# A two-block kernel: the input's pieces loaded in another order, and fourteen matmuls of ones at the head

## The chip, the core and the metric

One core of a Trainium2 chip runs the whole program. Its engines are TensorE (PE, matmuls; its weight loads are PEld), VectorE (DVE), ScalarE (ACT), GpSimd (POOL) and SyncE (SP, which issues most of the DMA transfers). Each engine works through its own list of instructions in order and waits at an instruction until what it needs is there. The metric is the device time of one execution, in microseconds (us). In the profiled execution the span, from the first instruction to the last, is a little shorter than that time.

## What is computed

The reference is two transformer-like blocks over 256 positions of width 1024, one after the other. Here matters the start of the first one:

```python
def first_block(x, mem, mix_norm_g, w_in, ...):
    ...
        h = _rmsnorm(x, mix_norm_g[l])
        proj = h @ w_in[l]
        u_s5, q_in, k_in, v_in, o_in, i_pre, f_pre, gate_pre = jnp.split(proj, split_points, axis=-1)
        y_s5 = _s5(u_s5, ...)          # complex diagonal scan, 32 groups of 64 states
        y_m = _mlstm(q_in, k_in, v_in, o_in, i_pre, f_pre, ...)   # gated matrix memory, 4 heads, 2 chunks of 128
        ...
        merged = g_s5 * (y_s5 @ w_br_s5[l]) + g_m * (y_m @ w_br_m[l])
        x = x + merged @ w_out[l]
        h = _rmsnorm(x, x_norm_g[l])
        x = x + _cross_attn(h, _rmsnorm(mem, mem_norm_g[l]), x_wq[l], x_wkv[l], x_wo[l])
        h = _rmsnorm(x, f_norm_g[l])
        x = x + _conv_ffn(h, f_w_up[l], f_conv_w[l], f_conv_b[l], f_w_down[l])
    return _rmsnorm(x, final_norm_g)
```

The second block has two layers of attention and convolution networks. All values are float32.

## The kernel before

Products with weights are made from pairs. `wload` (L313) fetches a weight tile by SP into `raw`, ScalarE casts it to `hi` (L321) and VectorE makes `lo` = raw - hi (L322). The activations have such a pair too, `xh` (ScalarE, L569) and `xl` (VectorE, L570). A product is then three matmuls, hi with xh, hi with xl, lo with xh: `fm_mm` (L329 to L331, the result has features on the partitions) and `tm_mm` (L338 to L340, it has positions there). The pool for `raw` has 4 buffers, those for `hi` and `lo` 3 each, and the PSUM tiles `g` for the results 3; `a` (4) and `m` (1) are the other PSUM tiles.

The head fetches the first weight tile in two halves of 512 columns and the input `x` in four pieces of 2 of its 8 slices (L1653 to L1667). `rms_defer` (L566) makes xh and xl from the unnormalised x, slice by slice, and squares, a sum by matmuls with a column of `ones` (`col_sums`, L455) and a broadcast (L499) for the norm's factor, which is multiplied in later where results leave PSUM (L1689, `msg`). The order of the first long part is then: products for the scan's input and for q and k (`w_fm`, L329 to L331, with the convolution L1695 to L1700 behind them), the scan's tables (VectorE's `so` and `hs`, L754 and L755; ScalarE's L764 to L790; TensorE's L779 to L787), products for v, the two gates and the output gate (`w_vif` and `w_tm`, L338 to L340; `ifs` at L1716, `vm` at L1714, `og` at L1729 and L1730), the scan's local sums (L805, evicted by ScalarE L806), the scan over time on VectorE (L815 to L818), and the mLSTM (from L888; per head L919, L928, ScalarE's `dm`, VectorE's `pT` L931, then L933 to L935; `hn` L951; L952), with further `w_fm` products, which need none of these, in between. The scan's output is L842, from 155 us.

The order of the instructions isn't the program's. `tile.TileContext(schedule_with_timeline_sim=True)` lets a scheduler place them by priorities and by a time that it computes itself, so a change of a priority, or of the work at the head, can move instructions far behind it. `tc.high_priority(n)` raises what stands under it by n; `wload` raises its own by `WPRI` = 300 within whatever stands around it.

Of the kernel before, what the change touches and what calls it, by code (L numbers as in the profile page):

```python
# [20 lines left out]
P = 128  # L21
# [10 lines left out]
WPRI = 300  # L32
# [220 lines left out]
def program(tc, nc, a, offs, dump=lambda n, t: None):  # L253
    with ExitStack() as ctx:
        _program(ctx, tc, nc, a, offs, dump)


def _program(ctx, tc, nc, a, offs, dump):
# [14 lines left out]
    pm = pool(ctx, "pm", 1, space=PSUM)  # L273
    cnt = [0]

    def T(pl, shape, tag, dt=F32, **k):
        cnt[0] += 1
        return pl.tile(list(shape), dt, tag=tag, name="%s_%d" % (tag, cnt[0]), **k)
# [6 lines left out]
    mm = PE.matmul  # L285
# [4 lines left out]
    ident = C["ident"]  # L290
    ones = T(cp, [P, P], "ones")
    G.memset(ones, 1.0)
    mhalf = T(cp, [P, 8], "mhalf")
    G.memset(mhalf, -0.5)
    zcol = T(cp, [P, 1], "zcol")
# [17 lines left out]
    def wload(name, i, c0=0, c1=None):  # L313
        src = a[name][i]
        src = src[:, c0:src.shape[-1] if c1 is None else c1]
        n = src.shape[-1]
        with tc.high_priority(WPRI):
            raw = T(wr, [P, n], "raw")
            nc.sync.dma_start(raw, src)
            hi, lo = [T(next(wp[s]), [P, n], s, F32R) for s in ("hi", "lo")]  # L320
            ACT.copy(hi, raw)  # L321
            tt(lo, raw, hi, op=sub)  # L322
        return hi, lo
# [1328 lines left out]
    with ExitStack() as ph:  # L1652
# [3 lines left out]
        with tc.high_priority(1000):  # L1656
            nc.scalar.dma_start(early, a["early"])

            first = []
            for half_ in range(2):  # L1660
                with tc.high_priority(4000 - WPRI):
                    first.append(wload("w_fm", 0, 512 * half_, 512 * half_ + 512))
                for k in range(2 * half_, 2 * half_ + 2):
                    with tc.high_priority(4000):
                        nc.sync.dma_start(x[:, 2 * k:2 * k + 2, :], a["x"][:, 2 * k:2 * k + 2, :])
            ahead = [([(0, 4), (4, 4)], first)]
            C.update({k: early[:, o:o + n] for k, (o, n) in off_e.items()})  # L1667
# [181 lines left out]
```

## Time and profile before

| what | value |
| --- | --- |
| time, median of 3 runs | 1207.07 us (1204.92 to 1209.34) |
| time of the profiled execution | 1207.08 us |
| its span | 1205.3 us |
| mean granted clock of TensorE | 0.991 |
| TensorE busy | 1165.0 us (97%) |
| VectorE busy | 888.5 us (74%) |
| ScalarE busy | 692.3 us (57%) |
| GpSimd busy | 73.1 us (6%) |

Busy times are sums over the span. An engine's share tells little of a stretch, as the stretches have different limits; a time outside the span (1207.08 - 1205.3 = 1.8 us) belongs to no instruction.

### The profile page before, as it was taken

Reading aid. Unit: us, or ns where it says so; the run is one execution under the profiler, and the core shown is the slowest. Engines: PE = TensorE matmul, PEld = TensorE weight load, DVE = VectorE, ACT = ScalarE, POOL = GpSimd, SP = SyncE. Lnnn points to the kernel's source line nnn. Section 1 sums busy time; section 2 is a strip of 40 time slices with the busy share of each in tenths; the row PEclk is TensorE's granted clock in tenths of the full one; section 3 lists DMA queues with packets and bytes.
Section 4 is the critical chain, followed back from the end, with each engine's and each line's share of the span. In section 5 each row is a group of like instructions: output and inputs, shape, how many; then the busy total and the mean of one; then the engine's idle time right before and its main releaser. Section 6 shows DMA issues by size and latency. Waiting matters only on the chain.

```text
span 1205.3 us, 23538 instructions
## 1 busy us (share of the span) xinstructions
PE 1165.0 (97%) x9370; PEld 1106.2 (92%) x9370; DVE 888.5 (74%) x1685; ACT 692.3 (57%) x1229; POOL 73.1 (6%) x80
## 2 busy tenths in 40 slices
PE   7899999999999999999999899999999999999997
PEld 7889989999999998899988899998988789999986
DVE  8979857866688887667565886666697868976654
ACT  5684645655565765446355675554686666755441
POOL 4400000100000000000001000001000001000010
PEclk9999999999999999999999999999999999999998
DMA  7524435654356556656433466666863225666561
GB/s 269 156 73 154 159 117 186 215 184 140 122 166 203 180 184 174 196 180 213 163 92 108 160 186 182 179 182 190 296 202 107 67 74 184 203 191 178 161 204 36
DMA packets 61276, 199.41 MB, mean 165 GB/s; under 512 B 8502, under 2 KB 12398, under 8 KB 60910
## 3 DMA queue, kind: packets, MB, share of 16 engines
q1 hardware_dynamic: 54864, 191.60, 50.1%
q10 hardware_dynamic: 6302, 6.32, 1.6%
q8 instruction: 73, 1.20, 0.4%
q14 instruction: 37, 0.30, 0.1%
HBM read 196.28 MB, written 1.60 MB: 164 GB/s over the span
## 4 chain that ended last, share of the span: by engine, by line
PE 87%; DVE 6%; ACT 3%; issue 2%; DMA 1%; POOL 1%; DVEq 0%; SPq 0%; ACTq 0%
PE g L330 12%; PE g L329 12%; PE g L331 12%; PE a L329 7%; PE a L330 7%; PE a L331 7%; PE a L394 5%; PE g L394 4%; PE a L396 3%; PE g L340 2%; PE g L338 2%; PE g L339 2%; DVE lo L322 2%; PE g L396 2%; PE m L1150 1%
## 5 line engine op out<-in xcount | busy, mean ns | idle before, releaser
L322 DVE TENSOR_TENSOR lo<-raw,hi 128x1024 fp32r<-128x1024 f32 (+3 forms) x359 | 428.4, 1199 | 181.9 <-ACT hi L321 179.5
L321 ACT CAST hi<-raw 128x1024 fp32r<-128x1024 f32 (+3 forms) x359 | 363.6, 1020 | 341.5 <-PE g L330 127.7
L329 PE MATMUL g<-xh,hi 128*128 128x256 f32 (+1 forms) x616 | 176.0, 286 | 8.3 <-ACT xh L569 8.0
L330 PE MATMUL g<-xl,hi 128*128 128x256 f32 (+1 forms) x624 | 178.3, 286 | 0.3
L331 PE MATMUL g<-xh,lo 128*128 128x256 f32 (+1 forms) x616 | 175.3, 285 | 1.4 <-DVE lo L322 1.4
L329 PE MATMUL a<-nh,hi 128*128 128x256 f32 x560 | 159.4, 285 | 4.7 <-ACT sqa L1075 2.8
L330 PE MATMUL a<-nl,hi 128*128 128x256 f32 x560 | 158.8, 284 | 0.9 <-DVE nl L517 0.9
L331 PE MATMUL a<-nh,lo 128*128 128x256 f32 x560 | 158.7, 284 | 0.0
L329 PEld LDWEIGHTS g<-xh,hi 128*128 128x128 f32 x616 | 117.2, 190 | 9.6 <-ACT xh L569 8.0
L330 PEld LDWEIGHTS g<-xl,hi 128*128 128x128 f32 x624 | 118.9, 190 | 1.6 <-DVE xl L570 0.8
L331 PEld LDWEIGHTS g<-xh,lo 128*128 128x128 f32 x616 | 116.9, 190 | 2.4 <-DVE lo L322 2.0
L329 PEld LDWEIGHTS a<-nh,hi 128*128 128x128 f32 x560 | 108.1, 193 | 5.7 <-ACT sqa L1075 2.9
L330 PEld LDWEIGHTS a<-nl,hi 128*128 128x128 f32 x560 | 108.1, 193 | 1.1 <-DVE nl L517 1.1
L331 PEld LDWEIGHTS a<-nh,lo 128*128 128x128 f32 x560 | 108.0, 193 | 0.0
L394 PE MATMUL a<-mx,hi 128*128 128x512 f32 x264 | 91.9, 394 | 0.0
L329 PE MATMUL g<-nh,hi 128*128 128x256 f32 x288 | 81.5, 283 | 0.0
L330 PE MATMUL g<-nl,hi 128*128 128x256 f32 x288 | 81.5, 283 | 0.0
L331 PE MATMUL g<-nh,lo 128*128 128x256 f32 x288 | 81.5, 283 | 0.0
L396 PE MATMUL a<-mx,lo 128*128 128x256 f32 x264 | 73.1, 277 | 0.0
L394 PE MATMUL g<-mx,hi 128*128 128x512 f32 x198 | 69.0, 395 | 0.0
L394 PEld LDWEIGHTS a<-mx,hi 128*128 128x128 f32 x264 | 49.4, 188 | 11.5
L329 PEld LDWEIGHTS g<-nh,hi 128*128 128x128 f32 x288 | 55.3, 192 | 0.0
(619 smaller groups left out, 2863.8 us busy)
## 6 DMA issues: line engine op xcount, KB each, us to landing
raw<-g_up SPq DMA_DIRECT2D x88, 512.0 KB, 3.6
raw<-f_up SPq DMA_DIRECT2D x44, 512.0 KB, 3.5
raw<-g_dn SPq DMA_DIRECT2D x32, 512.0 KB, 3.6
raw<-w_fm SPq DMA_DIRECT2D x27, 512.0 KB, 3.7
raw<-ev_fm SPq DMA_DIRECT2D x20, 512.0 KB, 3.7
raw<-f_dn SPq DMA_DIRECT2D x16, 512.0 KB, 3.5
raw<-od_fm SPq DMA_DIRECT2D x14, 512.0 KB, 4.4
raw<-g_dn SPq DMA_DIRECT2D x16, 384.0 KB, 3.3
```

Of the source, the lines that this page charges most:

```text
L321: ACT.copy(hi, raw)
L322: tt(lo, raw, hi, op=sub)
L329: mm(ps, hi[:, o:o + P], xh[:, k, :], start=start and k == 0, stop=False, skip_group_check=skip)
L330: mm(ps, hi[:, o:o + P], xl[:, k, :], start=False, stop=False, skip_group_check=skip)
L331: mm(ps, lo[:, o:o + P], xh[:, k, :], start=False, stop=stop and k == kt - 1, skip_group_check=skip)
L338: mm(ps, xh[:, k, t], hi[:, wsl], start=start and j == 0, stop=False, skip_group_check=skip)
L339: mm(ps, xh[:, k, t], lo[:, wsl], start=False, stop=False, skip_group_check=skip)
L340: mm(ps, xl[:, k, t], hi[:, wsl], start=False, stop=stop and j == len(ks) - 1, skip_group_check=skip)
L394: mm(f2, hi[:, o], X[:, k].rearrange("p a s -> p (a s)"), start=first and j == 0, stop=False, skip_group_check=True)
L396: mm(ps[:, 0, :], lo[:, o], X[:, k, 0, :], start=False, stop=last and j == len(ks) - 1, skip_group_check=True)
L1150: mm(o[64 * r:64 * r + 64, :], v0, pT[:, 0:S], start=first, stop=False, skip_group_check=True)
```

## The change

A PSUM tile `warm` is taken from the pool of `m`, and 14 matmuls of the tile `ones` (128x128, float32) with itself are written into it, as soon as `ones` is set; nothing reads it. And the priorities of the six transfers at the head change: the second half of the weight tile gets 100 less than the first, and each piece of x a number of its own, falling from the first to the last. Other numbers are not touched.

```diff
     ones = T(cp, [P, P], "ones")
     G.memset(ones, 1.0)
+    warm = T(pm, [P, P], "m")
+    for _ in range(14):
+        mm(warm, ones, ones, start=True, stop=True)
     mhalf = T(cp, [P, 8], "mhalf")
...
             for half_ in range(2):
-                with tc.high_priority(4000 - WPRI):
+                with tc.high_priority(4000 - 100 * half_):
                     first.append(wload("w_fm", 0, 512 * half_, 512 * half_ + 512))
                 for k in range(2 * half_, 2 * half_ + 2):
-                    with tc.high_priority(4000):
+                    with tc.high_priority(4000 + WPRI - 100 * half_ - 10 * k):
                         nc.sync.dma_start(x[:, 2 * k:2 * k + 2, :], a["x"][:, 2 * k:2 * k + 2, :])
```

The changed kernel has three lines more ahead of everything below, so L319 of before is L322 of the changed kernel, and so on.

The first place is the head. On SP's list, before (raw is the weight tile; the pieces of x were issued as slices 2 and 3 first, then 0 and 1, then 6 and 7, then 4 and 5):

```order
L319 DMA raw_108<-w_fm 128x512
L1665 DMA x_90<-x 128x512
L319 DMA raw_116<-w_fm 128x512
L1665 DMA x_90<-x 128x512 x3
L319 DMA raw_212<-w_fm 128x1024
L319 DMA raw_245<-w_fm 128x1024
L1669 DMA consts_91<-consts 128x914
```

and in the changed kernel:

```order
L322 DMA raw_123<-w_fm 128x512
L1668 DMA x_90<-x 128x512 x2
L322 DMA raw_131<-w_fm 128x512
L1668 DMA x_90<-x 128x512 x2
L322 DMA raw_227<-w_fm 128x1024
L322 DMA raw_260<-w_fm 128x1024
L1672 DMA consts_91<-consts 128x914
```

The piece that the second half of the weights followed is now two pieces, and they go out as slices 0 and 1, 2 and 3, 4 and 5, 6 and 7; everything behind row 6 keeps its order. ScalarE's list at the same place, from its first cast, before:

```order
L321 CAST hi_110<-raw_108 128x512
L569 ACTIVATE xh_139<-x_90,early_106 128x256 x2
L321 CAST hi_118<-raw_116 128x512
L569 ACTIVATE xh_139<-x_90,early_106 128x256 x2
L488 ACTIVATE sq_158<-x_90 128x512
L488 ACTIVATE sq_160<-x_90 128x512
L569 ACTIVATE xh_139<-x_90,early_106 128x256 x2
L492 ACTIVATE sq_27_164<-x_90 128x256
L492 ACTIVATE sq_28_166<-x_90 128x256
L569 ACTIVATE xh_139<-x_90,early_106 128x256 x2
L488 ACTIVATE sq_162<-x_90 128x512
L321 CAST hi_214<-raw_212 128x1024
```

and in the changed kernel:

```order
L324 CAST hi_125<-raw_123 128x512
L572 ACTIVATE xh_154<-x_90,early_121 128x256 x2
L491 ACTIVATE sq_173<-x_90 128x512
L572 ACTIVATE xh_154<-x_90,early_121 128x256 x2
L491 ACTIVATE sq_175<-x_90 128x512
L324 CAST hi_133<-raw_131 128x512
L572 ACTIVATE xh_154<-x_90,early_121 128x256 x2
L491 ACTIVATE sq_177<-x_90 128x512
L572 ACTIVATE xh_154<-x_90,early_121 128x256 x2
L495 ACTIVATE sq_28_179<-x_90 128x256
L495 ACTIVATE sq_29_181<-x_90 128x256
L324 CAST hi_229<-raw_227 128x1024
```

The same work stands ahead of the first full weight tile's cast (128x1024), in another order: the second half's cast comes after four xh and two squares instead of two xh.

The second place is TensorE where the last of the first five `w_fm` pairs of products ends (g_739 before, g_754 in the changed kernel), 47 us into the trace of before. TensorE's list before (g_904 is the first half of the positions of `w_vif`):

```order
L329 MATMUL g_739<-xh_139,hi_772 128x256
L330 MATMUL g_739<-xl_140,hi_772 128x256
L331 MATMUL g_739<-xh_139,lo_773 128x256
L779 MATMUL a_689<-consts_91,w_17_127 128x128 x4
L338 MATMUL g_904<-hi_908,xh_139 128x264
L339 MATMUL g_904<-lo_909,xh_139 128x264
L340 MATMUL g_904<-hi_908,xl_140 128x264
```

and in the changed kernel, with the products of `w_vif` (g_904 is now g_919) directly behind:

```order
L332 MATMUL g_754<-xh_154,hi_787 128x256
L333 MATMUL g_754<-xl_155,hi_787 128x256
L334 MATMUL g_754<-xh_154,lo_788 128x256
L341 MATMUL g_919<-hi_923,xh_154 128x264
L342 MATMUL g_919<-lo_924,xh_154 128x264
L343 MATMUL g_919<-hi_923,xl_155 128x264
```

The table's products L779 have moved behind the `w_vif` products. VectorE's list there, before, up to the `msg` (L1689) that reads g_507 and so frees the PSUM tile that g_904 takes (`so`, `hs` are the scan's tables):

```order
L1700 SCALAR_TENSOR_TENSOR x_431<-msg_504,mcv_495 128x512
L754 TENSOR_TENSOR so_814<-pz_350,cs_20_137 128x640
L322 TENSOR_TENSOR lo_957<-raw_954,hi_956 128x528
L755 TENSOR_TENSOR so_680<-so_680,hs_681 128x512
L1689 TENSOR_TENSOR msg_568<-g_507,rs_184 128x512
L754 TENSOR_TENSOR hs_815<-pz_350,cs_20_137 128x640
```

and in the changed kernel, up to the `ifs` (L1719, before L1716) for which the second half of the `w_vif` products waits; the `msg` for which the first half waits stands 13 rows above it:

```order
L325 TENSOR_TENSOR lo_972<-raw_969,hi_971 128x528
L757 TENSOR_TENSOR hs_687<-cz_389,cs_21_152 128x512
L1700 SCALAR_TENSOR_TENSOR mcv_585<-msg_583,consts_91,mcv_585 128x254 x2
L757 TENSOR_TENSOR so_695<-cz_389,cs_21_152 128x512
L758 TENSOR_TENSOR so_686<-so_686,hs_687 128x512
L1700 SCALAR_TENSOR_TENSOR mcv_585<-msg_583,consts_91,mcv_585 128x253
L1719 SCALAR_TENSOR_TENSOR ifs_914<-g_919,rmsr_194,consts_91 128x8
L1700 SCALAR_TENSOR_TENSOR mcv_585<-msg_583,consts_91,mcv_585 128x253
L757 TENSOR_TENSOR hs_696<-cz_389,cs_21_152 128x512
```

So `ifs` now stands about where `msg` stood.

The third place is TensorE around the scan's local sums, L805 (now L808). Before, the last of them and what follows; 119 `w_tm` products like those at the end stand between L805 and the mLSTM's L888:

```order
L805 MATMUL a_1003<-U_173_977,gs_429 128x64 x4
L805 MATMUL a_1003<-U_173_977,gm_430 128x64 x4
L805 MATMUL a_1013<-U_173_977,gs_429 128x64 x4
L805 MATMUL a_1013<-U_173_977,gm_430 128x64 x4
L339 MATMUL g_1023<-lo_1057,xh_139 128x256
L340 MATMUL g_1023<-hi_1056,xl_140 128x256
L338 MATMUL g_1023<-hi_1056,xh_139 128x256
```

In the changed kernel:

```order
L808 MATMUL a_998<-U_174_992,gs_444 128x64 x4
L808 MATMUL a_998<-U_174_992,gm_445 128x64 x4
L808 MATMUL a_1008<-U_174_992,gs_444 128x64 x4
L808 MATMUL a_1008<-U_174_992,gm_445 128x64 x4
L808 MATMUL a_1018<-U_174_992,gs_444 128x64 x4
L808 MATMUL a_1018<-U_174_992,gm_445 128x64 x4
L808 MATMUL a_1028<-U_174_992,gs_444 128x64 x4
L808 MATMUL a_1028<-U_174_992,gm_445 128x64 x4
L891 MATMUL m_1319<-lf_1317,cs_21_152 128x8
L892 MATMUL m_1319<-lf_1317,ones_92 128x4
L893 MATMUL m_1319<-ones_92,lf_1317 4x1
L333 MATMUL g_1504<-xl_155,hi_1507 128x256
```

All those 119 `w_tm` matmuls, and 4 of `w_fm`, stand ahead of L805 now; the mLSTM's L888 to L890 (now L891 to L893) follow it directly. On the way to VectorE's first L815 there are 14 rows more than before (5 `lo`, 4 `og`, 5 small ones), and on ScalarE's to its first L806 12 more (5 `hi`, 4 `og`, 2 `vm`, 1 `msg`). Before the first L842, TensorE's list holds the same work in both but for the 14 new matmuls and 4 `w_fm` ones.

## Rows read from the trace of the kernel before

**Rows 1.** The page: busy time by engine, and the chain that ended last.
```profile
PE 1165.0 (97%) x9370; PEld 1106.2 (92%) x9370; DVE 888.5 (74%) x1685; ACT 692.3 (57%) x1229; POOL 73.1 (6%) x80
...
PE 87%; DVE 6%; ACT 3%; issue 2%; DMA 1%; POOL 1%; DVEq 0%; SPq 0%; ACTq 0%
```

**Rows 2.** TensorE's timeline from 7 to 15 us: start, duration, instruction, idle before it.
```profile
8.01 0.58 PE L329 MATMUL g<-xh,hi 128*128 128x256 f32 x1 [8.01 <-ACT xh L569]
...
9.31 0.41 PE L329 MATMUL g<-xh,hi 128*128 128x256 f32 x1
...
13.40 0.28 PE L330 MATMUL g<-xl,hi 128*128 128x256 f32 x1
...
14.00 0.28 PE L329 MATMUL g<-xh,hi 128*128 128x256 f32 x1
...
14.23 0.28 PE L329 MATMUL g<-xh,hi 128*128 128x256 f32 x1
```

**Rows 3.** The chain of work that ended last, 0 to 75 us: start, duration, piece.
```profile
1.17 4.87 DMA x<-x
```

**Rows 4.** ScalarE's timeline from 0 to 14 us.
```profile
6.13 0.91 ACT L569 ACTIVATE xh<-x,early 128x256 fp32r<-128x256 f32 x2 [2.03 <-DMA x<-x]
...
12.03 1.98 ACT L321 CAST hi<-raw 128x1024 fp32r<-128x1024 f32 x2
```

**Rows 5.** TensorE's timeline at 21 us and from 51 to 55 us.
```profile
21.36 0.61 PE L499 MATMUL m<-consts,rmsr 128*128 128x128 f32 x4
...
51.42 0.56 PE L338 MATMUL g<-hi,xh 128*128 128x264 f32 x1 [3.74 <-DVE msg L1689]
...
51.99 0.42 PE L340 MATMUL g<-hi,xl 128*128 128x264 f32 x1
...
54.39 0.29 PE L339 MATMUL g<-lo,xh 128*128 128x264 f32 x1
```

**Rows 6.** Busy time in stretches, each engine's with its instructions; granted clock, DMA share.
```profile
14.00:45.00 31.00, 30.81 (x261) 30.59 (x260) 30.16 (x89) 15.23 (x20) 16.89 (x21) 1.00 0.69 205
...
50.00:55.00 5.00, 3.58 (x19) 3.61 (x19) 4.97 (x9) 4.10 (x8) 0.00 (x0) 0.66 0.58 221
45.00:76.30 31.30, 25.03 (x188) 22.45 (x187) 24.57 (x43) 27.24 (x55) 1.43 (x1) 0.95 0.31 97
60.00:65.00 5.00, 3.59 (x27) 2.95 (x25) 2.52 (x4) 4.86 (x12) 0.00 (x0) 1.00 0.00 0
85.00:135.00 50.00, 50.00 (x404) 48.18 (x402) 49.86 (x92) 25.41 (x49) 1.64 (x1) 1.00 0.42 138
135.00:155.00 20.00, 20.00 (x166) 19.54 (x165) 14.08 (x30) 12.24 (x29) 1.64 (x1) 1.00 0.54 174
```

**Rows 7.** TensorE's waits from 45 to 76 us: total, times, longest.
```profile
PE g L338 <- DVE msg L1689: 3.7, 1, 3.7
PE a L779 <- ACT w L772: 1.3, 1, 1.3
PE g L339 <- DVE lo L322: 1.1, 1, 1.1
```

**Rows 8.** VectorE's timeline from 50 to 96 us.
```profile
50.59 0.68 DVE L1689 TENSOR_TENSOR msg<-g,rs 128x512 f32<-128x512 f32 x1
...
77.21 1.22 DVE L322 TENSOR_TENSOR lo<-raw,hi 128x1024 fp32r<-128x1024 f32 x1
...
84.33 1.23 DVE L815 TENSOR_TENSOR w<-ST,ak 128x1024 f32<-128x1024 f32 x1
...
95.73 0.49 DVE L1730 TENSOR_SCALAR og<-og 128x256 f32<-128x256 f32 x2
```

**Rows 9.** TensorE's timeline: L805 from 76 us, and the first L842.
```profile
76.32 1.10 PE L805 MATMUL a<-U,gs 128*128 128x64 f32 x8
...
82.62 1.06 PE L805 MATMUL a<-U,gm 128*128 128x64 f32 x8
...
155.60 0.32 PE L842 MATMUL a<-U,KS 128*32 128x64 f32 x8
```


## The prediction

> **What bounds the kernel now.** I read the page first: TensorE is busy for 97% of the span, and 87% of the chain that ended last is its own [rows 1]. Its matmuls stay as they are, so time can only come out of what TensorE waits and out of what it does at half pace, and a change to the head can only move those. The timeline of the head shows the first wait: nothing runs until 8.01 us, and the matmuls up to 13.40 follow each other at the slower of the clock's two levels (0.41 us each, against 0.28 behind it) [rows 2]. The granted clock's column reads 1.00 there, so at the head the level is read from the matmuls' lengths alone. The windows then show where else TensorE idles: of 14 to 45 us it is busy for all but 0.19; of 45 to 76.3 it lacks 31.30 - 25.03 = 6.27; from 85 to 155 it lacks nothing [rows 6]. In that second stretch the waits name VectorE, ScalarE and VectorE again, 3.7, 1.3 and 1.1 us [rows 7], and behind the longest, at 51.42, thirteen matmuls run at the lower level (0.42 us, granted clock 0.66 in that window) [rows 5, 6]. VectorE has no idle time from 85 to 135 (49.86 of 50) and 20 - 14.08 = 5.92 from 135 to 155 [rows 6]. All that I expect lies between 45 and 155 us: behind the first L842 the lists of both kernels differ in a few neighbours only.
>
> **The head.** The first matmul needs slice 0. Its piece now goes out in the place of the piece issued at 1.17 and there 4.87 later, at 6.04 [rows 3]; its xh is half of the pair that takes 0.91 from 6.13 [rows 4]. So the first matmul can start near 6.7, 1.3 us earlier. The fourteen matmuls of ones: four records, which are two float32 matmuls of this size, take 0.61 us at the upper level [rows 5]. So one costs at most 0.3, fourteen 4.3 at the upper level, and at the lower, by the ratio of the steps below (0.218 / 0.12), some 8; without the pipeline's tail of each group (0.61 less 0.28, three steps of 0.11) they cost 3.1 and 5.6. From about 1 us, when `ones` is set, they end between 4.1 and 9, and I take 6.6, just ahead of the first real matmul. Even an end at 9 leaves the 24 matmuls ahead of the full tiles room up to the casts below (24 x 0.12 = 2.9, so 11.9).
>
> What does this lead reach? ScalarE works without a gap from 6.13 to 14.01, and the list of the change has the same work ahead of the full weight tiles' two casts, which take 1.98 from 12.03 [rows 4]. The matmul that needs the first of them now started at 14.00, the first that needs the second at 14.23 [rows 2]; the second cast ends at 14.01. The lead, whatever it was at 8 us, has shrunk there to 14.23 - 14.01 = 0.2. VectorE gets its input from the same casts and isn't earlier either. By 45 us TensorE waits for VectorE anyway. **I count the head at 0**, with bounds of 0 and 0.2.
>
> The Trainium skill (TensorE: Matmul & The Clock Gate, Part 1, What's actually happening) says that the throttled level is the default and that activity lifts it; its table Why this matters for your kernels advises matmuls ahead of those that count. The trace agrees that the first matmuls are slow, but by the sum above their pace isn't what ends last. By the rule alone the sum would have the head's 4.4 us of the third rival in place of 0.
>
> **45 to 76 us.** To be won are the 6.27 of idle time and the slow stretch: thirteen matmuls from 51.42 to 54.39 (2.97), which would take 13 x 0.12 = 1.6 at the upper step (0.12, from 13.40 to 14.00 [rows 2]; the lower is (54.39 - 51.99) / 11 = 0.218 [rows 5]), so 1.4, 7.7 in all. Now TensorE goes from `w_fm`, whose end is at 51.42 - 3.74 - 0.60 = 47.08, straight to 24 `w_vif` matmuls, as the `msg` that frees their tile stands 13 rows ahead of `ifs`. They take 24 x 0.12 = 2.9, to 50. Then it waits for `ifs`, which stands on VectorE about where `msg` stood, and that ended at 50.59 + 0.68 = 51.27 [rows 8]. With 0.5 for the rows by which the lists differ this is 51.8: a wait of 1.8 in place of 3.74, 1.9 won (bounds 0.9 and 2.9). The wait of 3.74 was followed by the slow level, the 1.3 at 62 us was not (1.00 in 60 to 65) [rows 6, 7]. 1.8 is nearer to the latter, so I count the 1.4 as won too. The other 2.5 of idle time meet `w_tm` products that stand ready, but each 24 of those want a `lo` that VectorE now has to make in the stretch where it is full: I take two fifths, 1.0 (0 to 2.5). **TensorE's lead when it comes to L805 is then 1.9 + 1.4 + 1.0 = 4.3**, with bounds of 0.9 (nothing but the lower end of the first) and 6.8, or 7.7 if no wait is left at all.
>
> **What is late for it.** 123 matmuls more, 123 x 0.12 = 14.8 us, stand ahead of L805 now. It began at 76.32 [rows 9], and will at 76.32 + 14.8 - 4.3 = 86.8, 10.5 later. VectorE's scan (L815) starts when the last of L805 is evicted: they ended at 82.62 + 1.06, and L815 began at 84.33 [rows 8, 9]. It starts 10.5 later too, at about 95. VectorE fills some of this with work that stood behind it: five `lo` of 1.22, four `og` of 0.25 and five small ones, which I take at 0.1 each, 6.1 + 1.0 + 0.6 = 7.7 [rows 8]. **So VectorE is 10.5 - 7.7 = 2.8 us late at the scan**, and being full to 135 it can't catch up before that; it has 5.92 of idle time after it. TensorE has spent its fillers early: of the `w_fm` products that stood between the mLSTM's steps, where it waits for `pT` and `hn`, some are gone ahead. Ends of the term: nothing is lost (the 5.92 takes it all), or all of the 2.8. For 135 to 155 the idle time was itself waiting on TensorE's and ScalarE's short steps, so I can't count it as free, and take the second.
>
> **Sum.** 4.3 - 2.8 = 1.5 us won when L842 begins (155.60 before), and kept to the end, where TensorE sets the pace. With the profiled execution's own time, 1207.08, which is that of the runs' median (1207.07): 1205.6. In general, the gain is the lead less (14.8 - lead - 7.7): twice the lead, less 7.1. That is 0 for a lead of 3.55.
>
> **Rivals.** 0.3% is 3.6 us, about what a measurement of this kernel can tell from no change.
> 1. The lead is kept: VectorE's lateness is wholly taken in by its idle 5.92. Then 1207.1 - 4.3 = 1202.8, and with the lead at its upper end, 6.8, 1200.3. For it speaks that TensorE lacked nothing from 85 to 155; against it, that VectorE then lacked nothing either to 135. It ends over 0.3% for leads over 3.6 in this case, and over 5.35 in the sum above.
> 2. Slower: the scan's delay is dearer than the lead. If the stalls at 47 to 76 return as waits for `lo`, with a lead of 1.7, L805 begins 13.1 later, VectorE is 5.4 late, and the time is 1207.1 - 1.7 + 5.4 = 1210.8. It decides from a lead below 1.75 (0.3%). For it: ScalarE is full in 60 to 65 (4.86 of 5) and now has 12 more rows ahead of the eviction; against: 5.92 to absorb it.
> 3. The head's own gain reaches the end: 1.3 of earlier start, and 13.40 - 8.01 = 5.39 of slow stretch with 19 matmuls that take 2.3 at the upper step, 3.1 less; together 4.4, so 1202.7. Against it stand the casts at 12.03 and the 1.8 of waiting for `ifs` that I still expect.
> 4. It does nothing: lead and delay cancel, 1207.
>
> **Chances.** The forecast with rival 4, which lie within 0.3%: 0.66; rival 1: 0.17; rival 3: 0.04; rival 2: 0.13. So faster 0.21, same 0.66, slower 0.13. The range of 8 in 10 takes in most of rivals 1 and 2: 1201.7 to 1209.7.
>
> **What would show it.** Of the changed trace: the first matmul of `w_fm` near 6.7 and at the upper level, but the 27th product at 14.0 or later; a wait near 50 us of 1 to 3 in place of 3.74, for `ifs`, with no slow stretch behind it; L805 at about 87; L815 at about 95 with idle time on VectorE just ahead of it; new waits of TensorE for `pT`, `hn` or `lo` between 105 and 155 of 2 to 4 us in all; L842 at about 154. The prediction is wrong if the waits ahead of L805 sum to more than 6 (slower), or if no wait comes between 105 and 155 (faster).

## The result, and the profile after

The changed kernel takes 1217.76 us (median of 9 runs, 1214.23 to 1219.78) against 1207.89 for the kernel before, measured beside it (9 runs, 1204.92 to 1211.95). The ratio is 1.0074, with an interval of 1.0063 to 1.0085: 9 us slower by the ratio, 9.9 between the medians, where 1.5 us less was forecast and the range ended at 1209.7. The profiled execution of it took 1215.1, near the lower end of its runs, with a span of 1213.3 (1205.3 before).

The page has, for its busy times and its chain (as [rows 1]):

```profile
PE 1175.3 (97%) x9398; PEld 1116.6 (92%) x9398; DVE 887.4 (73%) x1685; ACT 692.6 (57%) x1229; POOL 73.0 (6%) x80
...
PE 77%; DVE 3%; ACT 2%; issue 1%; POOL 0%; DVEq 0%; ACTq 0%
```

TensorE is busy for 10.3 us more, of which the ones are 4.9; the busy times of VectorE, ScalarE and GpSimd change by 1.1 at most. The rest goes with more time at the lower of the clock's two levels (mean granted clock 0.984, before 0.991). To see where the time goes, I took each matmul's start in this trace less that of the same one before (the n-th of its kind). The changed kernel is 1.9 us late at 20 us, 0.55 **early** from 173 to 207, 6.5 late from 232 to 615, 8.0 late at 640 and 7.9 at the end. So the stretch that the prediction was about ends with a small gain, and most of the loss, 7.0 us, falls between 207 and 232 us, which the prediction did not look at; 1.5 more come between 615 and 640.

The head, in TensorE's timeline (as [rows 2]; columns as there). L295 are the ones, two records to each:

```profile
0.99 4.92 PE L295 MATMUL m<-ones 128*128 128x128 f32 x28 [0.99 <-POOL ones L292]
5.98 0.38 PE L332 MATMUL g<-xh,hi 128*128 128x256 f32 x1
...
7.24 0.28 PE L334 MATMUL g<-xh,lo 128*128 128x256 f32 x1
...
11.68 0.58 PE L333 MATMUL g<-xl,hi 128*128 128x256 f32 x1 [0.99 <-DVE xl L573]
12.06 0.41 PE L334 MATMUL g<-xh,lo 128*128 128x256 f32 x1
...
14.62 0.48 PE L332 MATMUL g<-xh,hi 128*128 128x256 f32 x1
...
17.89 0.28 PE L332 MATMUL g<-xh,hi 128*128 128x256 f32 x1
```

The first product starts at 5.98 and the upper level is there (0.28 us). But now TensorE is ahead of what feeds it: it waits 0.65, 0.55, 0.42 and 0.99 us for xl and xh, and from 11.68 to 17.8 the matmuls take 0.41 again. The product that needs the second full tile's cast starts at 14.62, 0.4 later than before instead of 0.2 earlier. ScalarE, which now waits 1.06 us for a piece of x on the way, starts the two casts 0.46 later than before (12.03, [rows 4]):

```profile
7.90 0.91 ACT L572 ACTIVATE xh<-x,early 128x256 fp32r<-128x256 f32 x2 [1.06 <-DMA x<-x]
...
12.49 1.98 ACT L324 CAST hi<-raw 128x1024 fp32r<-128x1024 f32 x2
```

At 50 us, TensorE's timeline (as [rows 5]), then L805 and the first L842 (now L808 and L845, as [rows 9]):

```profile
54.37 0.39 PE L341 MATMUL g<-hi,xh 128*128 128x264 f32 x1 [2.29 <-DVE ifs L1719]
...
55.43 0.42 PE L343 MATMUL g<-hi,xl 128*128 128x264 f32 x1
...
88.15 1.00 PE L808 MATMUL a<-U,gs 128*128 128x64 f32 x8
...
158.00 0.32 PE L845 MATMUL a<-U,KS 128*32 128x64 f32 x8
```

VectorE's timeline at the scan (as [rows 8]):

```profile
95.96 0.17 DVE L895 COPY bcum<-m 128x8 f32<-128x8 f32 x1 [6.37 <-PE m L893]
96.06 1.22 DVE L818 TENSOR_TENSOR w<-ST,ak 128x1024 f32<-128x1024 f32 x1
```

TensorE's waits from 100 to 160 us (as [rows 7]):

```profile
PE a L955 <- DVE hn L954: 1.6, 1, 1.6
PE g L332 <- ACT x L957: 0.6, 1, 0.6
```

The wait for `ifs` is there (2.29), L805 starts at 88.15, the scan at 96.06 after 6.37 of idle time, and 2.1 us of waits for `hn` and x are new (1.56 and 0.56). The first L842 starts at 158.00, 2.4 later than before, and by 173 us the changed kernel is 0.55 early all the same. About 1.5 us of that turn is the clock: the changed kernel has a stretch at the lower level (0.41 us a matmul) from 154.4 to 157.8, ahead of the first L842, and the kernel before has one as long behind it, from 163.5 to 167. A line of the latter:

```profile
163.94 0.42 PE L330 MATMUL g<-x,hi 128*128 128x256 f32 x1
```

Then the place that decides. It is the end of the products with `w_out` and the start of the cross attention, which reads `mem`. TensorE's timeline there:

```profile
207.60 0.28 PE L334 MATMUL g<-xh,lo 128*128 128x256 f32 x1
211.91 0.39 PE L332 MATMUL g<-xh,hi 128*128 128x256 f32 x1 [4.03 <-ACT hi L324]
...
213.17 0.58 PE L334 MATMUL g<-xh,lo 128*128 128x256 f32 x1 [0.76 <-DVE lo L325]
213.55 0.42 PE L332 MATMUL g<-xh,hi 128*128 128x256 f32 x1
...
219.10 0.36 PE L334 MATMUL g<-xh,lo 128*128 128x256 f32 x1
```

TensorE waits 4.03 us for a cast and 0.76 for the `lo` made from it, and then 28 matmuls run at the lower level, up to 219. What holds up the cast stands in ScalarE's timeline of the changed kernel:

```profile
201.55 1.05 ACT L324 CAST hi<-raw 128x1024 fp32r<-128x1024 f32 x1 [1.78 <-PE g L333]
205.44 3.31 ACT L572 ACTIVATE oh<-mem,consts 128x256 fp32r<-128x256 f32 x8 [2.84 <-DMA mem<-mem]
208.66 1.65 ACT L491 ACTIVATE sq<-mem 128x512 f32<-128x512 f32 x3
210.21 0.71 ACT L495 ACTIVATE sq<-mem 128x256 f32<-128x256 f32 x2
210.82 2.93 ACT L324 CAST hi<-raw 128x1024 fp32r<-128x1024 f32 x3
```

and, of the kernel before, in the same view:

```profile
202.05 1.05 ACT L321 CAST hi<-raw 128x1024 fp32r<-128x1024 f32 x1 [1.73 <-PE g L330]
204.95 2.00 ACT L321 CAST hi<-raw 128x1024 fp32r<-128x1024 f32 x2 [1.85 <-PE g L330]
206.85 3.31 ACT L569 ACTIVATE oh<-mem,consts 128x256 fp32r<-128x256 f32 x8
```

Before, two casts of `w_out` stood ahead of `mem`'s eight scalings (`oh`) and five squares. Now they stand behind them: ScalarE stops at the first `oh` for the transfer of `mem` (2.84 us), works off 3.31 + 1.65 + 0.71, and only then casts, while TensorE waits. ScalarE's list shows it, before (52 casts stand ahead of the `oh`):

```order
L321 CAST hi_2616<-raw_2614 128x1024
L321 CAST hi_2648<-raw_2646 128x1024
L321 CAST hi_2678<-raw_2676 128x1024
L569 ACTIVATE oh_2784<-mem_2782,consts_91 128x256 x8
```

and now (50 of them):

```order
L324 CAST hi_2631<-raw_2629 128x1024
L572 ACTIVATE oh_2799<-mem_2797,consts_91 128x256 x8
L491 ACTIVATE sq_2818<-mem_2797 128x512
L491 ACTIVATE sq_2820<-mem_2797 128x512
L491 ACTIVATE sq_2822<-mem_2797 128x512
L495 ACTIVATE sq_442_2824<-mem_2797 128x256
L495 ACTIVATE sq_443_2826<-mem_2797 128x256
L324 CAST hi_2663<-raw_2661 128x1024
L324 CAST hi_2693<-raw_2691 128x1024
```

### The profile page after: what moved, and what is told of

Its sections match the earlier page's. It is cut to its first block, busy times and chain, and to the rows that moved or that the text cites. A ratio compares the mean times of both kernels' runs of the same rounds, so it can differ in the third digit from the quotient of the medians.

```text
span 1213.3 us, 23592 instructions
## 1 busy us (share of the span) xinstructions
PE 1175.3 (97%) x9398; PEld 1116.6 (92%) x9398; DVE 887.4 (73%) x1685; ACT 692.6 (57%) x1229; POOL 73.0 (6%) x80
## 4 chain that ended last, share of the span: by engine, by line
PE 77%; DVE 3%; ACT 2%; issue 1%; POOL 0%; DVEq 0%; ACTq 0%
PE g L333 10%; PE g L332 10%; PE g L334 10%; PE a L332 7%; PE a L333 7%; PE a L334 7%; PE a L397 5%; PE g L397 4%; PE a L399 3%; PE g L399 2%; PE g L343 2%; PE g L341 2%; PE g L342 2%; PE m L1153 1%; PE a L964 1%; DVE lo L325 1%
```

## Experiments

**Theory A:** the loss is this swap on ScalarE, which the scheduler made 200 us behind the edit. **Theory B:** the ones and what they do to the clock cost it, at the head and behind. Ratios are to the kernel before on the same chip.

**1. No ones.** The list of every other instruction is row for row that of the changed kernel, so the new order comes from the transfers' priorities alone, and the ones can be tried by themselves.

```diff
-    warm = T(pm, [P, P], "m")
-    for _ in range(14):
-        mm(warm, ones, ones, start=True, stop=True)
```

> The changed kernel without its fourteen matmuls of ones; the order of everything else is row for row the same. Theory A (the loss sits at 205 to 220 us, where two of the last casts of w_out stand behind the eight oh and five squares on ScalarE): same time as the changed kernel, 1216 to 1218, with the wait of about 4.0 us near 207 still there; the head alone differs. Theory B (the ones themselves cost it: after them TensorE is fed in drops, the clock falls at 10.3 us and stays low to about 17): 1210 or less, since the slow stretch at 11.7 to 17 us goes.

Measured: 1215.28, ratio 1.0053 (1.0039 to 1.0066), 0.7 us under the range that A gave. The wait near 207 is there:

```profile
PE g L329 <- ACT hi L321: 3.8, 1, 3.8
```

Most of the loss stays without the ones, so B fails as its main cause. Whether the ones have a part in the 2.5 us between the ratios 1.0053 and 1.0074 this run doesn't settle.

**2. The swap undone.** `tc.issue_after` orders the issue on one engine and waits for nothing else.

```diff
...
+        with tc.issue_after(w_out_casts[5].ins):
-        ms_, mc_ = rms_defer(mem, 8, C["mem_norm_g"], 1e-6, memh, meml)
+            ms_, mc_ = rms_defer(mem, 8, C["mem_norm_g"], 1e-6, memh, meml)
```

`w_out_casts` lists the casts of `w_out` in their order.

> The changed kernel, with mem's eight oh and five squares queued on ScalarE behind the sixth cast of w_out, as in the kernel before; ones and new order of x stay. From the end of the first block's scan on the order is that of before, TensorE's few matmuls around 155 us apart. Theory A: the 7 us at 207 to 220 go, and the 1.5 at 620 us that came with the same shift: 1207 to 1208.5. Theory B: 1215 or more, only the wait at 207 moves elsewhere.

Measured: 1207.76, ratio 0.9992 (0.9983 to 1.0001). All of the loss is gone. SP's transfers stand in the changed kernel's order, and that of `mem` is issued at 200.60 us (200.58 there), so the transfer by itself isn't the cause. TensorE's waits from 200 to 228 us are one line, where the changed kernel has 4.0 and 0.8:

```profile
PE g L338 <- DVE lo L329: 0.4, 1, 0.4
```

**3. The swap alone, in the kernel before.** Two casts are queued behind `mem`'s squares there; up to 205 us the lists of ScalarE and VectorE are those of before.

```diff
...
         ms_, mc_ = rms_defer(mem, 8, C["mem_norm_g"], 1e-6, memh, meml)
+        tc.add_manual_dep(w_out_casts[4].ins, squared[0].ins.name,
+                          mybir.DependencyInfo(mybir.DependencyClass.NoSync, mybir.DependencyReason.DATA),
+                          reason="issue_after")
```

`squared` holds the last square of `mem`; the dependency orders the issue alone.

> The kernel before, with the fifth and sixth cast of w_out queued on ScalarE behind mem's squares, as the changed kernel has it; no ones, old order of x. Theory A: 6 to 8 us slower than before, 1214 to 1216, with a wait of TensorE for hi of 3 to 5 us near 208 and low-clock matmuls behind it. Theory B: within 2 us of before, 1206 to 1210.

Measured: 1215.06, ratio 1.0054 (1.0042 to 1.0067). TensorE's timeline of it has the same picture, and its matmuls are 0.5 us early at 204 and 6.3 late at 233:

```profile
212.27 0.58 PE L333 MATMUL g<-xh,hi 128*128 128x256 f32 x1 [4.39 <-ACT hi L323]
...
213.53 0.58 PE L335 MATMUL g<-xh,lo 128*128 128x256 f32 x1 [0.46 <-DVE lo L326]
```

**4. Twice the ones.**

```diff
-    for _ in range(14):
+    for _ in range(28):
```

> The changed kernel with 28 matmuls of ones in place of 14; the order of everything else is row for row the same. Fourteen took 4.92 us and end at 5.9; 28 end near 9 (the last half at the upper level). Theory A: within 1 us of the changed kernel, 1216.5 to 1219, as the casts at 12 to 14 us decide at the head. Theory B: a different time by 2 us or more, faster if the upper level holds through 14 us, slower if the first real matmul is only held up to 9.

Measured: 1214.32, ratio 1.0042 (1.0029 to 1.0054). The ones take 9.47 us, the first product starts at 10.22, later than before, and from there all run at the upper level, with one wait of 0.44 for a cast. The product that needs the second full tile starts at 14.27. Most of the loss stays, again against B as the main cause. But my expectation for A (within 1 us of fourteen) was missed by 2.2 us, and the difference of 2 us or more that I gave to B did show: 3.9 us by the ratios, 2.8 against the fourteen of run 5. This trace is 3.0 us ahead of the first one of the changed kernel from 60 to 130 us.

**5. The changed kernel once more,** unedited, beside the next three.

> The changed kernel as it stands, for a direct comparison with the three beside it. Theory A (the casts of w_out behind mem's work): 1214 to 1218, ratio to before 1.005 to 1.008. Nothing else is asked of it.

Measured: 1216.44, ratio 1.0065 (1.0050 to 1.0080).

**6 and 7. The swap undone, with 28 ones and with none.** The edits of 2 and 4, and of 2 and 1, together.

> The changed kernel with 28 ones and with mem's work queued behind the sixth cast of w_out. Theory A plus what the trace with 28 ones showed (TensorE 3.0 us ahead of the changed kernel from 60 us, kept to 690): the head's 3.0 to 3.4 and the 7 us both come back: 1204 to 1205.5, that is 2.5 to 4.5 us less than before. Rival (the lead is lost again at 155 or 207 us, where the order waits for VectorE or ScalarE anyway): within 1 us of the same kernel with 14 ones, 1207 to 1209.

> The order of x alone: the changed kernel without ones, with mem's work queued behind the sixth cast of w_out. By the trace without ones (0.4 to 1.2 us ahead of the changed kernel between 20 and 600 us) fourteen ones cost more than they give: 1206 to 1208, 0.5 to 1.5 us less than before. If the ones give their 1 to 2 us of pace, it is 1208.5 to 1210 instead.

Measured: 1207.39, ratio 0.9985 (0.9976 to 0.9994), with 28 ones, which is the rival's time and not A's; 1208.47, ratio 0.9998 (0.9990 to 1.0007), with none, where 0.5 to 1.5 us less than before was expected. With the swap undone, none, 14 and 28 ones give 0.9998, 0.9992 and 0.9985; with the swap 1.0053, 1.0065 and 1.0042. The intervals that lie next to each other overlap, so no effect of the ones is settled; the 2.5 to 4.5 us that I expected of 28 came out as 1.8. The kernel of 6 is the only one here whose interval lies below the kernel before; its ratio is 0.15% under it.

**8. The ones alone,** with the transfers' old priorities. The scheduler again moves the first 160 us, but leaves the two casts ahead of `mem`.

```diff
     G.memset(ones, 1.0)
+    warm = T(pm, [P, P], "m")
+    for _ in range(14):
+        mm(warm, ones, ones, start=True, stop=True)
```

> The fourteen ones alone: the kernel before with them, with its old order of the transfers. The scheduler places the first 160 us anew, much as in the changed kernel, but ScalarE casts the sixth tile of w_out ahead of mem's work, as before. Theory A: no wait of 4 us near 207, so 1206.5 to 1209, the same as before within 0.2%. Theory B (the ones, or the new order of the first 160 us, cost the time): 1212 or more.

Measured: 1209.25, ratio 1.0008 (0.9996 to 1.0019), within the 0.2% that A gave, and TensorE's wait is not there (0.4 for a `lo`). The ones and a moved first 160 us cost nothing that shows, though up to 0.19% isn't excluded.

**9. Half of the swap.** Only `mem`'s squares go behind the two casts, the `oh` stay ahead.

```diff
-        r = rms_cols(x, kt, eps, at)
+        with tc.issue_after(behind) if behind else ExitStack():
+            r = rms_cols(x, kt, eps, at)
...
-        ms_, mc_ = rms_defer(mem, 8, C["mem_norm_g"], 1e-6, memh, meml)
+        ms_, mc_ = rms_defer(mem, 8, C["mem_norm_g"], 1e-6, memh, meml,
+                             behind=w_out_casts[5].ins)
```

> The changed kernel with mem's five squares (2.2 us) queued behind the two casts of w_out, and the eight oh still ahead of them. Theory A gives a size: the casts start at 208.7 in place of 210.8 and TensorE waits 1.9 us for them in place of 4.03. If the low-clock stretch behind the wait (28 matmuls, 2.7 us) stays, 4.9 us remain of the 7: 1212.5 to 1214; if the shorter wait keeps the upper level, 2 us remain: 1209.5 to 1211. A rival for the cause (something else than the queue, such as mem's transfer taking bandwidth at that place): no change, 1216.

Measured: 1211.63, ratio 1.0019 (1.0002 to 1.0035), 2.3 us over before in place of 8 to 9. That is between the two sizes that A gave, with runs from 1205.91 to 1214.37, so it doesn't tell them apart. ScalarE's timeline, and TensorE's wait:

```profile
197.30 1.05 ACT L326 CAST hi<-raw 128x1024 fp32r<-128x1024 f32 x1 [1.75 <-PE g L337]
204.03 3.30 ACT L576 ACTIVATE oh<-mem,consts 128x256 fp32r<-128x256 f32 x8 [5.68 <-DMA mem<-mem]
207.24 1.98 ACT L326 CAST hi<-raw 128x1024 fp32r<-128x1024 f32 x2
...
208.32 0.58 PE L336 MATMUL g<-xh,hi 128*128 128x256 f32 x1 [4.69 <-ACT hi L326]
```

In this execution TensorE came to the place 4.2 us earlier than in the first trace of the changed kernel, the work on `mem` only 1.4 (204.03 for 205.44; 7.7 us after the transfer was issued, 4.9 there). So TensorE's wait was 4.69 and not the 1.9 expected: 1.9 + 4.2 - 1.4 = 4.7. The place cost this execution as much as the changed kernel, 7.2 us (4.8 early at 204, 2.4 late at 233). So the lower median doesn't show that the loss falls with the work in the queue; that stays open.

**10. All eight casts ahead of `mem`,** with 28 ones (index 7 in place of 5 in the edit of 2).

> 28 ones, and mem's work queued behind all eight casts of w_out in place of six. If the two waits of 0.5 us that the kernel before has behind 213 us come from the last two casts, 0.5 to 1 us less than with six: ratio to before 0.9975 to 0.9982. If mem's work is then late for the keys (TensorE needs oh from 225 us on), slower than with six by 1 us or more.

Measured: 1207.20, ratio 0.9989 (0.9976 to 1.0001). No different from six casts; the 0.5 to 1 us expected didn't show.

## Why the prediction was wrong

**The step that failed** is the sentence that behind the first L842 "the lists of both kernels differ in a few neighbours only", and with it "kept to the end, where TensorE sets the pace". The lists do differ little there. But one of the differences puts two casts behind thirteen instructions on ScalarE, the first of which waits for a transfer. I took differences for harmless because they were few, and never asked what stands in the queue between the places exchanged. The rows for it were at hand: 3.31 + 1.65 + 0.71 of work, and a cast that TensorE's next product needs behind it. The price in the first trace: 4.03 + 0.76 of waiting, against 0.5 for a `lo` at this place before, and the slow stretch, 28 matmuls that take 0.10 us more each, 2.8; together 7.1, where the comparison of starts has 7.0 (0.55 early to 6.5 late). Experiments 2 and 3 show this from both sides: without the swap no loss, with the swap alone 0.54%. And by the comparison of starts at 204 and 233 us the place costs 6.8 to 7.2 us in each of the six traces with the swap or half of it (the changed kernel, 1, 3, 4, 5, 9), nothing in 2, 6, 7 and 8, and 0.4 in 10.

**The rest of the 9 us.** Another 1.5 come at 615 to 640 us in the first trace. There the order of both kernels differs as well, and the order of before returns in experiment 2. But in the traces of 6, 7, 8 and 10, which have that order, matmuls run at the lower level there too; in those of the kernel before, 2, 3 and 9 they don't. With the changed kernel's order it came in each of four traces (the first, 1, 4 and 5). Whether order or chance decides there stays open. By the runs, the swap alone (1.0054) and the change (1.0065 and 1.0074) differ by less than their intervals can settle.

**The head.** Counted at 0, it was 1.9 us late up to 35 us and 1.35 at 47 in the first trace. The casts at 14 us did take the lead away, as the sum had it, and came 0.46 later besides: "the same work ahead" now holds a wait for x. What the sum also lacked was that TensorE, started early and fed in drops, can fall back to the lower level, and that the products behind the casts then run slowly (11.68 to 17.8), 1.5 of the 1.9. After fourteen ones and four waits of 0.42 to 0.99 us the clock fell in this execution, after 28 ones and one wait of 0.44 it did not. The Trainium skill (TensorE: Matmul & The Clock Gate, Why this matters for your kernels) warns of long idle gaps between bursts of matmuls. The trace agrees at 207 us, where the lower level follows a wait of 4.03; at the head it came after gaps of less than 1 us, of which the table says nothing. In the trace of experiment 5, the same kernel, it held through waits of 0.60, 0.41 and 1.00 (the matmuls behind take 0.28, and the granted clock is 1.00 over the first 20 us, last section), so the waits alone don't decide it.

**45 to 155 us** went by the steps, but not by their sizes. The wait is for `ifs`, 2.29 for the 1.8 foretold. The 1.4 of the slow stretch came back in this execution (0.42 us at 55.43), against "I count the 1.4 as won too". L805 started at 88.15 (86.8 foretold), so the lead was 14.8 - (88.15 - 76.32) = 3.0 in place of 4.3: less by the head's 1.35 and the slow stretch's 1.4, more by 0.8 of idle time won (TensorE idles 2.55 us from 45 to 88.15, so 6.27 - 2.55 = 3.7 for the 2.9 counted); 0.6 stay unexplained. The scan came at 96.06 (95), with VectorE idle 6.37 ahead of it. The new waits were for `hn` and x, 2.1 in all; x wasn't named, and `hn` alone, 1.6, is under the 2 to 4 foretold. The first L842 came at 158.00 where 154 was foretold, so the 1.5 "won when L842 begins" was 2.4 lost in this trace. Of these, 1.5 are a slow stretch that stands ahead of L842 now and stood behind it before; at 173 us, when both kernels have had theirs, 0.55 is won. The rest of that turn lies within L842's products, and its cause stays open. In the traces of 5 and 9, where the clock held to 62 us, L805 started at 85.50 and 84.12 and L842 at 154.95 and 153.49. So the mechanism held, and the terms that were mis-sized are the lead and the slow stretch in it. (The sum also has a slip: five small ones at 0.1 are 0.5 and not 0.6, so 1.4 us won and not 1.5; nothing hangs on it.)

**The rivals.** All four stood ahead of 155 us; none held the case. The second came nearest, being on the right side, but for another reason: the loss lies 50 us behind the scan. The prediction's own sign of a slower kernel, more than 6 us of waits ahead of L805, did not come (2.55); it looked only ahead of 155 us.

## What to carry to other kernels

Where a scheduler decides the order, look for the change's cost at every place where the two lists differ, however far from the edit, and price each by what the exchanged instructions wait for and who waits behind them: two casts put behind a wait for a transfer and 5.7 us of other work cost 7 us here, 200 us after the last line that was edited. And a lead that is won early need not reach the end. With the swap undone, the traces of 6, 7 and 10 are 2.6, 3.9 and 4.9 us ahead of the kernel before at 204 us, and 2.5, 3.8 and 4.5 at 600. At 1000 they are 1.0 late, 0.2 late and 0.4 ahead, with the lower level coming more often on the way: granted clock 0.96 in 600 to 640, 0.83 in 680 to 700 and 0.89 in 900 to 930 us in all three, against 1.00, 0.91 and 0.94 before. Why it comes more often there no run shows. Of all that lead 0.15% at most is left in the times.

## What the runs showed of the hardware

The clock's lower level comes and goes between executions of one and the same list. Three traces share the changed kernel's order over their first 150 us: the first, experiment 5 and experiment 9. In windows of 0 to 20 and 45 to 62 us, where the last three columns are granted clock, DMA share and GB/s, they show, in this order:

```profile
0.00:20.00 20.00, 16.19 (x87) 15.00 (x88) 15.66 (x38) 11.89 (x20) 12.64 (x16) 0.83 0.82 293
45.00:62.00 17.00, 14.45 (x105) 13.66 (x104) 16.75 (x28) 13.91 (x24) 6.19 (x11) 0.90 0.41 137
```

```profile
0.00:20.00 20.00, 16.39 (x99) 14.97 (x99) 16.12 (x39) 12.00 (x20) 12.63 (x16) 1.00 0.86 289
45.00:62.00 17.00, 14.42 (x117) 13.51 (x117) 16.74 (x28) 14.01 (x26) 5.02 (x8) 1.00 0.43 142
```

```profile
0.00:20.00 20.00, 16.91 (x110) 15.70 (x111) 17.42 (x48) 12.14 (x22) 13.29 (x17) 1.00 0.85 312
45.00:62.00 17.00, 14.44 (x117) 13.38 (x116) 16.74 (x28) 14.00 (x26) 3.72 (x6) 1.00 0.40 141
```

Compared matmul by matmul, the second and third are 1.25 and 2.64 us ahead of the first at 30 us, and 2.65 and 4.03 at 60. The wait of 2.3 us for `ifs` was followed by the lower level in the first and not in the others. So a forecast of a microsecond at such a place holds for some executions only, and one trace can't size it.
